# A softmax over 16 tiles: whole-tile passes, long multiplies, a later alignment, two stores from another issuer

## Chip, cores, metric

One core of one Trainium2 chip. The metric is the device time in microseconds (us) of one execution; medians over several executions are quoted.

Engine names as in the profile: DVE is VectorE, ACT is ScalarE, POOL is GpSimd, SP is SyncE; a q behind a name (SPq) is that engine's sequencer.

## The reference

```python
x = randn(32, 512, 1024) as float32        # 64 MiB in, 64 MiB out
scaled = x / 0.5
shifted = scaled - max(scaled, axis=-1)
out = exp(shifted) / sum(exp(shifted), axis=-1)
```

## The kernel before

The 16384 rows are 16 tiles of 128 partitions x 8 rows x 1024 elements, 4 MiB each, computed in place in six buffers. SP issues the loads, ACT the stores. Each tile is worked in two groups of four rows.

```python
TILES = [[8]] * 16
BUFS = 6
GROUP = 4
# ... cut: building the list of groups, the DRAM views
def load():                                # SP; waits until the buffer's old store has landed
    xt = data.tile([P, sum(TILES[i]), d], f32, name="xt")
    nc.sync.dma_start(out=xt, in_=dram(xf, i))
def maximum(g):                            # DVE
    nc.vector.tensor_reduce(out=top, in_=tiles[i][:, a : a + k, :], axis=X, op=extreme)
    nc.vector.tensor_scalar_mul(bias, in0=top, scalar1=-scale)
def exponential(g):                        # ACT, row by row, with the sum
    nc.scalar.activation(row, row, Exp, bias=bias[:, b : b + 1], scale=scale,
                         accum_out=sums[:, b : b + 1])
def divide(g):                             # DVE, row by row
    nc.vector.reciprocal(recip, sums)
    for b in range(k):
        nc.vector.tensor_scalar_mul(row, in0=row, scalar1=recip[:, b : b + 1])
def store(g):                              # ACT issues, once a tile
    nc.scalar.dma_start(out=dram(of, i)[:, a : a + k, :], in_=tiles[i][:, a : a + k, :])
    load()                                 # the load of tile i + 6

nc.vector.addr_align(128, offset=0, max_nops=0)
nc.scalar.addr_align(128, offset=0, max_nops=0)
for _ in range(BUFS):
    load()
for g in range(len(groups) + 1):           # one group ahead
    if g < len(groups):
        maximum(g); exponential(g)
    if g > 0:
        divide(g - 1); store(g - 1)
```

Of the kernel before, what the change touches and what calls it, by code (L numbers as in the profile page):

```python
# [1 line left out]

# [4 lines left out]



TILES = [[8]] * 16  # L10
BUFS = 6

GROUP = 4


@with_exitstack
def kernel(
    ctx: ExitStack,
    tc: tile.TileContext,
    x: bass.AP,  # L20
    temperature: bass.AP,
    out: bass.AP,
):
    nc = tc.nc
    f32 = mybir.dt.float32
    scale = 1.0 / float(temperature)
    extreme = mybir.AluOpType.max if scale > 0 else mybir.AluOpType.min

    P = 128
    xf = x.flatten_outer_dims()  # L30
    of = out.flatten_outer_dims()
    n, d = xf.shape
    assert sum(sum(ks) for ks in TILES) * P == n

    data = ctx.enter_context(tc.tile_pool(name="data", bufs=BUFS))
    stats = ctx.enter_context(tc.tile_pool(name="stats", bufs=4))


    groups, first, r = [], [], 0
    for i, ks in enumerate(TILES):  # L40
        first.append(r)
        r += sum(ks)
        a = 0
        for k in ks:
            for b in range(0, k, GROUP):
                m = min(GROUP, k - b)
                groups.append((i, a + b, m, (a, k) if b + m == k else None))
            a += k

    def dram(t, i):  # L50
        k = sum(TILES[i])
        block = t[P * first[i] : P * (first[i] + k), :]
        return block.rearrange("(p k) d -> p k d", p=P, k=k)

    tiles, small = [], []

    def load():
        i = len(tiles)
        if i < len(TILES):
            xt = data.tile([P, sum(TILES[i]), d], f32, name="xt")  # L60
            nc.sync.dma_start(out=xt, in_=dram(xf, i))
            tiles.append(xt)

    def maximum(g):
        i, a, k, _ = groups[g]
        top, bias, sums, recip = (
            stats.tile([P, k], f32, name=name) for name in ("top", "bias", "sums", "recip")
        )
        small.append((bias, sums, recip))
        nc.vector.tensor_reduce(  # L70
            out=top, in_=tiles[i][:, a : a + k, :], axis=mybir.AxisListType.X, op=extreme
        )
        nc.vector.tensor_scalar_mul(bias, in0=top, scalar1=-scale)  # L73

    def exponential(g):
        i, a, k, _ = groups[g]
        bias, sums, _ = small[g]
        for b in range(k):
            nc.scalar.activation(  # L79
                tiles[i][:, a + b, :],  # L80
                tiles[i][:, a + b, :],
                mybir.ActivationFunctionType.Exp,
                bias=bias[:, b : b + 1],
                scale=scale,
                accum_out=sums[:, b : b + 1],
            )

    def divide(g):
        i, a, k, _ = groups[g]
        _, sums, recip = small[g]  # L90
        nc.vector.reciprocal(recip, sums)  # L91
        for b in range(k):
            nc.vector.tensor_scalar_mul(  # L93
                tiles[i][:, a + b, :], in0=tiles[i][:, a + b, :], scalar1=recip[:, b : b + 1]
            )

    def store(g):
        i, _, _, part = groups[g]
        if part:
            a, k = part  # L100
            nc.scalar.dma_start(out=dram(of, i)[:, a : a + k, :], in_=tiles[i][:, a : a + k, :])
            if a + k == sum(TILES[i]):
                load()



    with tc.manual_schedule():

        nc.vector.addr_align(128, offset=0, max_nops=0)
        nc.scalar.addr_align(128, offset=0, max_nops=0)  # L110
        for _ in range(BUFS):
            load()
        for g in range(len(groups) + 1):
            if g < len(groups):
                maximum(g)
                exponential(g)
            if g > 0:
                divide(g - 1)
                store(g - 1)


# [1 line left out]
_INS = ['x', 'temperature']  # L123
_OUTS = [((32, 512, 1024), 'float32')]

_NUMBERS = {'temperature': 0.5}


# [26 lines left out]
```

## Time and profile before

| | before |
|---|---|
| median time | 317.70 us (317.50 to 317.98, 6 runs) |
| span of the profiled run | 315.6 us |
| DVE, ACT busy | 235.5 us, 149.6 us |
| DMA | 134.26 MB, 425 GB/s over the span |
| tile 15 lands, last store issued, last store landed | 282.23, 302.01, 314.82 us |

Read it from the DMA row down: the 16 DMA engines are at 9 tenths in 38 of the 40 slices, and DVE and ACT at 75% and 47% of the span.

### The profile page before, as it was taken

What the parts mean: (1) busy time and instruction counts of PE and PEld (TensorE: products, weight loads), DVE (VectorE), ACT (ScalarE), POOL (GpSimd) and SP (SyncE); (2) the same over time, 40 slices, a digit from 0 to 9 for tenths busy, and PEclk for the clock granted to TensorE, in tenths of its full rate; (3) what the DMA queues carried; (4) which work ended last, traced back from release to release, by engine and by line L of the source; (5) the groups of instructions that cost most, each with busy time, mean ns of one, the idle gap of its engine ahead of it and who ended that gap; (6) DMA issues with size and microseconds to landing.
All of it is one profiled execution on the core that took longest, in us unless ns stands there. A gap on an engine that the chain in (4) does not pass through costs nothing.

```text
span 315.6 us, 622 instructions
## 1 busy us (share of the span) xinstructions
DVE 235.5 (75%) x224; ACT 149.6 (47%) x257; POOL 0.2 (0%) x4
## 2 busy tenths in 40 slices
DVE  0299999999789494994939949498594976949720
ACT  0176666666626255361553615546065560645500
POOL 0000000000000000000000000000000000000000
DMA  8999999999999999999999999999999999999996
GB/s 330 415 448 415 386 457 407 461 411 453 424 440 432 432 432 429 444 424 453 415 454 407 457 407 457 403 461 403 461 403 461 403 462 403 461 419 444 428 436 278
DMA packets 4613, 134.26 MB, mean 425 GB/s; under 512 B 512, under 2 KB 512, under 8 KB 512
## 3 DMA queue, kind: packets, MB, share of 16 engines
q1 hardware_dynamic: 2304, 67.11, 49.7%
q10 hardware_dynamic: 2304, 67.11, 49.2%
q14 instruction: 5, 0.04, 0.0%
HBM read 67.11 MB, written 67.11 MB: 425 GB/s over the span
## 4 chain that ended last, share of the span: by engine, by line
DVE 72%; another core or an unknown queue 15%; DMA 4%; ACT 3%; issue 1%; DVEq 0%
DVE top L70 43%; DVE xt L93 27%; DMA xt<-in_x_dram 4%; ACT xt L79 3%; DVE recip L91 1%; DVE bias L73 1%; DVEq L150 0%
## 5 line engine op out<-in xcount | busy, mean ns | idle before, releaser
L79 ACT ACTIVATE xt<-xt,bias 128x1024 f32<-128x1024 f32 x128 | 145.4, 1137 | 136.0 <-DVE recip L91 118.6
L70 DVE TENSOR_REDUCE top<-xt 128x4 f32<-128x4096 f32 x32 | 141.3, 4416 | 62.2 <-DMA xt<-in_x_dram 62.2
L93 DVE TENSOR_SCALAR xt<-xt,recip 128x1024 f32<-128x1024 f32 x128 | 87.7, 749 | 1.1
L79 ACT ACTIVATION_READ_ACCUMULATOR xt<-xt,bias 128x1 f32 x128 | 23.8, 186 | 0.0
L79 ACT ACT_TABLE_LOAD x1 | 1.3, 1283 | 13.5 <-DMA xt<-in_x_dram 13.5
L91 DVE RECIPROCAL recip<-sums 128x4 f32<-128x4 f32 x32 | 5.5, 171 | 2.1 <-ACT xt L79 2.1
L73 DVE TENSOR_SCALAR bias<-top 128x4 f32<-128x4 f32 x32 | 5.5, 170 | 1.1
L136 POOL MEMSET const-bfloat16-1.0<- 128x1 bf16 x1 | 0.1, 102 | 0.0
L136 POOL MEMSET const-uint8-127<- 128x1 uint8 x1 | 0.1, 102 | 0.0
L136 POOL MEMSET const-float32-0.0<- 128x1 f32 x1 | 0.1, 99 | 0.2 <-issue 0.2
L136 POOL MEMSET const-float32-1.0<- 128x1 f32 x1 | 0.1, 99 | 0.0
## 6 DMA issues: line engine op xcount, KB each, us to landing
xt<-in_x_dram SPq DMA_DIRECT2D x16, 4096.0 KB, 50.2
out_dram<-xt ACTq DMA_DIRECT2D x16, 4096.0 KB, 38.4
```

The costliest lines, as they stand in the source:

```text
L70: nc.vector.tensor_reduce(out=top, in_=tiles[i][:, a : a + k, :], axis=mybir.AxisListType.X, op=extreme)
L73: nc.vector.tensor_scalar_mul(bias, in0=top, scalar1=-scale)
L79: nc.scalar.activation(tiles[i][:, a + b, :], tiles[i][:, a + b, :], mybir.ActivationFunctionType.Exp, bias=bias[:, b : b + 1], scale=scal ...
L91: nc.vector.reciprocal(recip, sums)
L93: nc.vector.tensor_scalar_mul(tiles[i][:, a + b, :], in0=tiles[i][:, a + b, :], scalar1=recip[:, b : b + 1])
L136: nc = _bacc.Bacc("TRN2", target_bir_lowering=False, num_devices=1)
```

## The change

The intent: fewer DVE instructions and waits (maximum over a whole tile in tiles 2 to 13; in six of these one long multiply by a broadcast operand in place of eight short ones), the two alignment instructions behind the fourth pass in place of the front, and the last two stores issued by SP, whose last load goes out at 231.9 us in the old trace.

```diff
-TILES = [[8]] * 16
-GROUP = 4
+PASSES = [[4, 4]] * 2 + [[8]] * 12 + [[4, 4]] * 2
+WHOLE = (3, 5, 7, 9, 11, 13)
+ALIGNED = 3
+BY_SP = 2
 ... (cut: the list of groups follows PASSES)
     def divide(g):
         nc.vector.reciprocal(recip, sums)
+        if i in WHOLE:
+            xt = tiles[i][:, a : a + k, :]
+            nc.vector.tensor_mul(xt, xt, recip.unsqueeze(2).to_broadcast([P, k, d]))
+            return
         for b in range(k):
             nc.vector.tensor_scalar_mul(...)
     def store(g):
-            nc.scalar.dma_start(...)
+        if a + k == ROWS:
+            queue = nc.scalar if i < len(PASSES) - BY_SP else nc.sync
+            queue.dma_start(out=dram(of, i), in_=tiles[i])
+            load()
     with tc.manual_schedule():
-        nc.vector.addr_align(128, offset=0, max_nops=0)
-        nc.scalar.addr_align(128, offset=0, max_nops=0)
         ...
                 store(g - 1)
+            if g == ALIGNED:
+                nc.vector.addr_align(128, offset=0, max_nops=0)
+                nc.scalar.addr_align(128, offset=0, max_nops=0)
```

More of the change, by code (lines that the diff above doesn't have):

```diff
@@ L6 @@
 from concourse._compat import with_exitstack
-TILES = [[8]] * 16
+ROWS = 8
 BUFS = 6
-GROUP = 4
+PASSES = [[4, 4]] * 2 + [[8]] * 12 + [[4, 4]] * 2
+WHOLE = (3, 5, 7, 9, 11, 13)
+ALIGNED = 3
+BY_SP = 2
 @with_exitstack
@@ L32 @@
     n, d = xf.shape
-    assert sum(sum(ks) for ks in TILES) * P == n
+    assert len(PASSES) * ROWS * P == n
     data = ctx.enter_context(tc.tile_pool(name="data", bufs=BUFS))
     stats = ctx.enter_context(tc.tile_pool(name="stats", bufs=4))
-    groups, first, r = [], [], 0
-    for i, ks in enumerate(TILES):
-        first.append(r)
-        r += sum(ks)
-        a = 0
-        for k in ks:
-            for b in range(0, k, GROUP):
-                m = min(GROUP, k - b)
-                groups.append((i, a + b, m, (a, k) if b + m == k else None))
-            a += k
+    groups = []
+    for i, ks in enumerate(PASSES):
+        assert sum(ks) == ROWS
+        for j, k in enumerate(ks):
+            groups.append((i, sum(ks[:j]), k))
     def dram(t, i):
-        k = sum(TILES[i])
-        block = t[P * first[i] : P * (first[i] + k), :]
-        return block.rearrange("(p k) d -> p k d", p=P, k=k)
+        block = t[P * ROWS * i : P * ROWS * (i + 1), :]
+        return block.rearrange("(p k) d -> p k d", p=P, k=ROWS)
     tiles, small = [], []
@@ L58, in load @@
         i = len(tiles)
-        if i < len(TILES):
-            xt = data.tile([P, sum(TILES[i]), d], f32, name="xt")
+        if i < len(PASSES):
+            xt = data.tile([P, ROWS, d], f32, name="xt")
             nc.sync.dma_start(out=xt, in_=dram(xf, i))
@@ L64, in maximum @@
     def maximum(g):
-        i, a, k, _ = groups[g]
+        i, a, k = groups[g]
         top, bias, sums, recip = (
@@ L75, in exponential @@
     def exponential(g):
-        i, a, k, _ = groups[g]
+        i, a, k = groups[g]
         bias, sums, _ = small[g]
@@ L88, in divide @@
     def divide(g):
-        i, a, k, _ = groups[g]
+        i, a, k = groups[g]
         _, sums, recip = small[g]
         nc.vector.reciprocal(recip, sums)
+        if i in WHOLE:
+            xt = tiles[i][:, a : a + k, :]
+            nc.vector.tensor_mul(xt, xt, recip.unsqueeze(2).to_broadcast([P, k, d]))
+            return
         for b in range(k):
@@ L97, in store @@
     def store(g):
-        i, _, _, part = groups[g]
-        if part:
-            a, k = part
-            nc.scalar.dma_start(out=dram(of, i)[:, a : a + k, :], in_=tiles[i][:, a : a + k, :])
-            if a + k == sum(TILES[i]):
-                load()
+        i, a, k = groups[g]
+        if a + k == ROWS:
+            queue = nc.scalar if i < len(PASSES) - BY_SP else nc.sync
+            queue.dma_start(out=dram(of, i), in_=tiles[i])
+            load()
     with tc.manual_schedule():
-        nc.vector.addr_align(128, offset=0, max_nops=0)
-        nc.scalar.addr_align(128, offset=0, max_nops=0)
         for _ in range(BUFS):
```

## The prediction

> **What bounds the kernel now.** I read the page's slices and DMA queues first, then the windows by stage, then the chain of waits, then the groups.
>
> From the page:
>
> ```profile
> span 315.6 us, 622 instructions
> DVE 235.5 (75%) x224; ACT 149.6 (47%) x257; POOL 0.2 (0%) x4
> ...
> DMA  8999999999999999999999999999999999999996
> ...
> DMA packets 4613, 134.26 MB, mean 425 GB/s; under 512 B 512, under 2 KB 512, under 8 KB 512
> q1 hardware_dynamic: 2304, 67.11, 49.7%
> q10 hardware_dynamic: 2304, 67.11, 49.2%
> q14 instruction: 5, 0.04, 0.0%
> ```
>
> No compute engine is full (DVE, VectorE, is busy 75% of the span), but the 16 DMA engines are at 9 tenths in every slice except the first and the last, and the loads (q1) and the stores (q10) together take 49.7 + 49.2 = 98.9% of them. That names the bound: bytes. Nothing in the program can remove bytes, since 67.11 MB must be read and 67.11 MB written.
>
> The windows by stage give the rate (columns: window, its length, busy time of DVE, ACT and POOL with their counts, clock, DMA share, GB/s):
>
> ```profile
> 14.00:32.00 18.00, 17.65 (x15) 11.65 (x20) 0.00 (x0) 1.00 1.01 437
> 32.00:40.00 8.00, 7.93 (x9) 5.25 (x11) 0.00 (x0) 1.00 1.00 389
> ...
> 88.00:282.00 194.00, 147.26 (x140) 92.74 (x160) 0.00 (x0) 1.00 1.01 434
> ```
>
> Loads alone run at 437 GB/s while DVE is busy 17.65 of 18 us, and loads mixed with stores run at 434. So the rate depends neither on the mix nor on what DVE does. Only the 8 us around the first store are slower, at 389: (434 - 389) / 434 of 8 us is 0.8 us lost.
>
> The chain of waits tells which engine waits in the steady part:
>
> ```profile
> 258.42 4.46 another core or an unknown queue
> ...
> 262.90 4.43 DVE top L70
> 267.35 0.17 DVE bias L73
> ...
> 282.25 4.43 DVE top L70
> ```
>
> DVE waits some 4.5 us for every tile, and tiles come 282.25 - 262.90 = 19.35 us apart. A tile is 4.194 MB in and 4.194 MB out; 8.389 MB in 19.35 us is 433.5 GB/s: the pace is the DMA's. The page's chain gives 72% to DVE, but that is only because it walks through an engine that itself waits for loads.
>
> The groups (count, then busy time and mean ns) give the durations that I use:
>
> ```profile
> L79 ACT ACTIVATE xt<-xt,bias 128x1024 f32<-128x1024 f32 x128 | 145.4, 1137 | 136.0 <-DVE recip L91 118.6
> L70 DVE TENSOR_REDUCE top<-xt 128x4 f32<-128x4096 f32 x32 | 141.3, 4416 | 62.2 <-DMA xt<-in_x_dram 62.2
> L93 DVE TENSOR_SCALAR xt<-xt,recip 128x1024 f32<-128x1024 f32 x128 | 87.7, 749 | 1.1
> ```
>
> [...] The trace shows that issue time as 0.34 us for a store. So moving two stores to SP (SyncE) is worth tenths at most. [...] four multiplies of 1024 elements take 2.74 us in the chain, 0.685 us each[...]. The new operation is in no trace yet[...]. [...] the store at 289.76 us was issued by ACT (ScalarE) before the last exponential of its group began (290.37).
>
> **The change part by part.**
> *Whole-tile passes (12 tiles).* A maximum over 8 rows replaces two over 4: 8192 elements in place of twice 4096. From the chain, 4.34 us for 4096, so about 8.6 to 8.75 for 8192; one bias and one reciprocal fewer a tile (0.17 + 0.09 us). DVE saves about 0.3 us a tile. But latency grows: the store of a tile now waits for the maximum of the whole next tile. Old: 4.43 + 0.17 + 0.09 + 2.74 = 7.4 us after the next tile's landing (7.5 in the trace, 282.25 to 289.76). New: 8.75 + 0.26 + 8 x 0.685 = 14.5 us[...].
> *Six tiles multiplied in one instruction.* 8.7 in place of 5.5 us: +3.2 us of DVE each, 19 us in all; the store of such a tile comes 8.75 + 0.26 + 8.7 = 17.7 us after the next landing.
> *Is DVE then the bound?* 14.5 us for plain tiles, 17.7 for the six, against tiles coming each 19.35 us: no. DVE's busy time becomes about 235.5 + 19 - 12 x 0.3 = 251 us.
> *Do buffers stall the loads?* A buffer's turn has 6 x 19.35 = 116 us. Held now: 19.35 (until the next landing) + 7.5 = 27 us; the rest, 89 us, is queueing in the two DMA queues (median 50.2 for a load, 38.4 for a store). New hold: 34 to 37 us, leaving 79 us or more, where a load and a store that share the engines need about 19.35 each. The queues get shorter but don't run dry.
> *Alignment and fewer instructions.* DVE runs 78 fewer: 12 x (1 reduction + 1 bias + 1 reciprocal) = 36, and 6 x 7 = 42 multiplies. The page has 5 instruction fetches of 8 KB (q14). Each takes one of the 16 engines for 8 KB at 434 / 16 GB/s = 0.3 us, and the slowest engine sets the end. One or two fewer: -0.3 to -0.6 us.
> *Last two stores by SP.* Same bytes, same engines: 0 to -0.3 us.
> *The first stores.* Old: store 0 issued at 33.1, store 1 at 47.9, and the load that waits for store 0 goes out at 57.3. So the store queue never ran dry. New: the first four passes are the old ones, then comes the maximum over 8 rows: 40.4 + 8.75 + 0.26 + 2.74 = 52.2 us[...]. That is just before store 0's end (57): most likely no gap; if there is one, the loads get the engines meanwhile, and only a second start of writing can cost its 0.8 us. I count a third of it, +0.2.
> *The tail.* If tile 15 still lands at 282.25: tile 14's four steps with tile 13's long multiply in between end at 262.90 + 4.43 + 0.26 + 8.7 + 4.34 + 0.26 + 2.74 = 283.6; then maximum, bias and reciprocal, multiply (7.34 us) to 291.0, maximum, bias, reciprocal and multiply again (7.34) to 298.3. The last exponentials end at about 300.2 and the last multiply, with its reciprocal, at about 303.1, where it was 302.0. Store 14 landed at 305.2 in the old trace, so the last store may be late by about a microsecond and still find the engines busy. And loads get ahead while early stores are later, so tile 15 should land up to 3 us sooner, which gives this back. Net 0.
> Sum: -0.45 - 0.1 + 0.2 + 0 = about -0.4 us: 317.7 - 0.4 = 317.3 us.
>
> **The rivals.**
> *DVE takes over.* For: +19 us of DVE work, and the catching-up between 13 and 85 us where DVE never waits. Against: 17.7 < 19.35. It would need a long multiply above 19.35 - 9.0 = 10.3 us[...]; at 13 us the six tiles would lose 6 x 2.7 = 16 us less the slack of the plain tiles (4.8 us each), so still only a few us: 319 to 322.
> *The tail opens.* The last store late by 2 to 3 us beyond what is queued: 319 to 320. For it: the shift of 1.1 us above. Against it: store 14's queue and the earlier loads.
> *A real gain.* The floor: 134.26 MB at 434 GB/s is 309.4 us; the first bytes come after some 1.5 us, and landing and closing take some 1.5 us: span 312.4, and 317.7 - 315.6 = 2.1 us lie outside the span: 314.5. That is 1.0% under now. A gain of over 2% (under 311.4) is not to be had without fewer bytes.
>
> **Range and chances.** 317.3 us; the sum's terms are each below a microsecond, the floor 314.5 closes it below, and the tail or the second start of writing can add 1 to 1.5: 316.0 to 318.8 for 8 in 10. Faster by over 2%: 0.01. Within 2%: 0.97. Slower by over 2% (above 324): 0.02[...].
>
> **What would show it.** Right: the DMA row stays at 9 throughout and the steady window at 434 GB/s; one group of six multiplies near 8.7 us; reductions of 128x8192 near 8.75; DVE near 251 us (80%) and still waiting for loads; stores issued 14 to 18 us after the next landing, landing sooner after issue than 38.4 us. Wrong: a slice at 8 or less in the DMA row between 40 and 300 us, SP waiting for stores with no load in flight, a gap between the landing of store 14 and the first bytes of store 15, or DVE without waits in the second half.

The sum: it came to -0.45 - 0.1 + 0.2 + 0 = -0.35, put as about -0.4 us, so 317.3 us. The 8.7 us for one long multiply, which is in the 17.7 us, in DVE's 251 us and in the tail, could not be had from the old trace (the changed kernel's shows 8692 ns). The -0.1 us for the last two stores is a guess beside the 0.34 us that issuing a store took in the trace. The floor holds for the measured 434 GB/s; that no more is to be had was not shown. Its two times of some 1.5 us are 1.74 us (the first data packet's start) and 1.1 us (315.6 - 314.47, from the last packet's end) in the old trace.

## More of the kernel before

All runs here were with a granted clock of 1.0.

"In the flow" means: while loads and stores keep all 16 DMA engines busy.

## The result, and the profile after

The changed kernel takes 318.23 us (317.78 to 318.49, 6 runs) where the old one takes 317.70. The ratio is 1.0014, 95% interval 1.0001 to 1.0027. Ratios here are the mean time of one kernel's fast runs over that of the other's in the same rounds, so not quite the ratio of the medians. It is the same within 2%, inside the predicted range, but on the other side: +0.5 us where -0.4 was predicted. The rest of this document is about that half microsecond; it is small, but most of it can be followed in the records.

The page of the changed kernel:

```profile
span 316.5 us, 534 instructions
DVE 250.8 (79%) x146; ACT 148.2 (47%) x257; POOL 0.2 (0%) x4
...
DMA  8999999999999999999999999999999999999996
...
q14 instruction: 5, 0.04, 0.0%
```

DVE has 15.3 us more work, and the DMA row is the same, digit for digit. There are 78 DVE instructions fewer, and still five instruction fetches.

Its windows by stage (window, length, busy time of DVE, ACT and POOL, clock, DMA share, GB/s):

```profile
32.00:40.00 8.00, 7.93 (x9) 5.25 (x11) 0.00 (x0) 1.00 1.00 385
...
88.00:282.00 194.00, 161.04 (x80) 87.89 (x153) 0.00 (x0) 1.00 1.01 434
```

The steady rate is 434 GB/s again. Nothing was gained or lost in those 194 us.

Its groups, shape by shape:

```profile
L70 DVE TENSOR_REDUCE top<-xt 128x8 f32<-128x8192 f32 x12 | 104.2, 8685 | 31.3 <-DMA xt<-in_x_dram 31.3
L94 DVE TENSOR_TENSOR xt<-xt,recip 128x8192 f32<-128x8192 f32 x6 | 52.1, 8692 | 0.2
```

Both durations are as forecast (8.6 to 8.75 us, from the old trace's 4.34 for half of it, and 8.7 us).

The end of its chain of waits (start, length, what):

```profile
258.24 4.92 another core or an unknown queue
...
263.19 4.43 DVE top L70
...
267.95 8.69 DVE xt L94
...
276.64 4.34 DVE top L70
...
284.03 4.34 DVE top L70
```

DVE waits for tile 14's landing (the 4.92 us), but not for tile 15's: that tile landed at 282.51, and its maximum starts at 284.03, because tile 13's 8.69 us stand in front. So the last store is issued at 303.63, where it was 302.01. The DMA engines notice. Microsecond by microsecond, before and then after:

```profile
303.00:304.00 1.00, 0.00 (x0) 0.00 (x0) 0.00 (x0) 1.00 1.22 524
304.00:305.00 1.00, 0.00 (x0) 0.00 (x0) 0.00 (x0) 1.00 1.14 492
```

```profile
303.00:304.00 1.00, 0.60 (x1) 0.00 (x0) 0.00 (x0) 1.00 0.31 131
304.00:305.00 1.00, 0.00 (x0) 0.00 (x0) 0.00 (x0) 1.00 1.22 524
```

A packet counts in the microsecond in which it starts, and takes 1.21 us; so shares go above 1, and a single thin microsecond can also be the space between two bunches of starts. The packet records settle it: from 302 to 309 us an engine idles 0.00 us on average before the change and 0.75 us after it, with only 3 of 16 engines active at the worst point. A gap near the very end, and 0.9 us more span: it looks like the whole explanation.

A second difference is quieter: where the instruction fetches (q14) fall. The queues in the first 10 us and from 10 to 313 us, before:

```profile
q1 hardware_dynamic: 110, 3.60, 89.9%
q14 instruction: 2, 0.02, 0.6%
...
q14 instruction: 3, 0.02, 0.0%
```

and after, for the same two stretches:

```profile
q1 hardware_dynamic: 108, 3.54, 88.7%
...
q14 instruction: 5, 0.04, 0.0%
```

Two of the five fetches have moved from the start into the flow, to 43.2 us. The trace shows the alignment as one branch instruction each on ACT and DVE: at 0.72 and 0.76 us before, at 37.42 and 37.50 after, some 6 us ahead of the two fetch packets.

### The profile page after: what moved, and what is told of

Read it like the earlier page. It is cut to its first block, busy times and chain, and to the rows that moved or that the text cites. A ratio compares the mean times of both kernels' runs of the same rounds, so it can differ in the third digit from the quotient of the medians.

```text
span 316.5 us, 534 instructions
## 1 busy us (share of the span) xinstructions
DVE 250.8 (79%) x146; ACT 148.2 (47%) x257; POOL 0.2 (0%) x4
## 4 chain that ended last, share of the span: by engine, by line
DVE 77%; another core or an unknown queue 11%; DMA 4%; ACT 3%; issue 1%; DVEq 0%; ACTq 0%
DVE top L70 43%; DVE xt L94 16%; DVE xt L97 16%; DMA xt<-in_x_dram 4%; ACT xt L79 3%; DVE recip L91 1%; DVE bias L73 1%; DVEq L154 0%; ACTq L154 0%
## 5 line engine op out<-in xcount | busy, mean ns | idle before, releaser
L70 DVE TENSOR_REDUCE top<-xt 128x8 f32<-128x8192 f32 (+1 forms) x20 | 139.5, 6976 | 49.4 <-DMA xt<-in_x_dram 49.4
L97 DVE TENSOR_SCALAR xt<-xt,recip 128x1024 f32<-128x1024 f32 x80 | 54.3, 748 | 0.5
L94 DVE TENSOR_TENSOR xt<-xt,recip 128x8192 f32<-128x8192 f32 x6 | 52.1, 8692 | 0.2
L91 DVE RECIPROCAL recip<-sums 128x8 f32<-128x8 f32 (+1 forms) x20 | 3.7, 185 | 2.0 <-ACT xt L79 2.0
L73 DVE TENSOR_SCALAR bias<-top 128x8 f32<-128x8 f32 (+1 forms) x20 | 3.4, 170 | 0.7
## 6 DMA issues: line engine op xcount, KB each, us to landing
out_dram<-xt ACTq DMA_DIRECT2D x14, 4096.0 KB, 28.8
```

What stands on the lines that cost most here:

```text
L94: nc.vector.tensor_mul(xt, xt, recip.unsqueeze(2).to_broadcast([P, k, d]))
L97: nc.vector.tensor_scalar_mul(tiles[i][:, a + b, :], in0=tiles[i][:, a + b, :], scalar1=recip[:, b : b + 1])
```

## The experiments

All runs gave correct results. They ran in three groups, in the order below (the first four, the next four, the last three), each with the old kernel beside it: its medians were 317.69, 317.72 and 317.81 us, so times from different groups compare to about 0.1 us.

**Theory T**: the gap in the tail. **Rival A**: the new issuer of the last stores. **Rival B**, later sharpened to **theory F**: the instruction fetches, which each set back one DMA engine, while the engine furthest back sets the end.

### Tile 13 short again (closes the gap)

```diff
-WHOLE = (3, 5, 7, 9, 11, 13)
+WHOLE = (3, 5, 7, 9, 11)
```

> The changed kernel with tile 13 multiplied by eight short instructions again (the other five long ones, SP's two stores and the moved alignment stay). Theory T (the tail: tile 13's long multiply, 8.69 us in place of 5.39, makes VectorE reach tile 15 at 284.0 us, 1.5 us after its landing at 282.5; so the last store is issued at 303.6 and the DMA engines idle about 1 us between stores 14 and 15): VectorE waits for tile 15 again, the last store goes out at 302.0 to 302.4, the window 303 to 304 us is full (over 400 GB/s, it was 131), and the time falls to 317.5 to 317.8, a ratio to before of 0.999 to 1.001. Rivals A (stores by SP) and B (alignment and instruction fetches): it stays at 318.2, ratio 1.0014.

Measured: 318.07 us, ratio to before 1.0011 (0.9999 to 1.0024). T misses. DVE waits for tile 15 again, and the microsecond from 303 is full:

```profile
303.00:304.00 1.00, 0.00 (x0) 0.00 (x0) 0.00 (x0) 1.00 1.15 492
304.00:305.00 1.00, 0.00 (x0) 0.00 (x0) 0.00 (x0) 1.00 0.15 66
```

The second line is mostly the space between two bunches: the packet records leave 0.25 us of idleness per engine, a third of the changed kernel's 0.75. It is not quite zero, as in this run tile 15 itself landed late, at 283.17, and the last store went out at 302.96. Taking away most of the gap gave 0.2 us at most, within the noise.

### The last two stores by ACT

```diff
-BY_SP = 2
+BY_SP = 0
```

> The changed kernel with the last two stores issued by ACT, as before. Theory T: the last store waits for VectorE's last multiply, whoever issues it, so it goes out at 303.6 plus or minus 0.2 us, the gap of about 1 us stays, and the time stays at 318.0 to 318.4. Rival A (a change of issuer[...] costs time): it falls to 317.7.

Measured: 318.30 us, ratio 1.0014 (1.0000 to 1.0027); the last store at 303.48. Rival A is out: the issuer is worth nothing that can be seen.

### Alignment at the front

```diff
     with tc.manual_schedule():
+        nc.vector.addr_align(128, offset=0, max_nops=0)
+        nc.scalar.addr_align(128, offset=0, max_nops=0)
 ...
-            if g == ALIGNED:
-                (both alignments)
```

> The changed kernel with the two alignment instructions at the front, as before. Theory T: the gap in the tail stays, time 318.0 to 318.4; the two instruction fetches seen at about 43 us move to the first 4 us. Rival B (placing of the fetches costs the time): it falls to 317.7 or moves by more than 0.4 us.

Measured: 317.74 us, ratio 0.9996 (0.9984 to 1.0009): the whole loss is gone. And the gap is still there, with the last store at 303.38:

```profile
303.00:304.00 1.00, 0.36 (x1) 0.00 (x0) 0.00 (x0) 1.00 0.16 66
```

The packet records have 0.64 us of idleness per engine, nearly the changed kernel's 0.75, and it costs nothing. T falls as the explanation of this half microsecond.

### Tile 14 long as well (a dose for the tail)

```diff
-WHOLE = (3, 5, 7, 9, 11, 13)
+WHOLE = (3, 5, 7, 9, 11, 13, 14)
```

> The changed kernel with tile 14 long as well (two instructions of 4 x 1024 elements, about 4.4 us each in place of 2.74). A dose: theory T says that each microsecond by which VectorE's last multiply is late beyond the edge is one microsecond of time. Both long multiplies stand before tile 15's last steps, +3.3 to +3.4 us: last store at about 307.0, DMA idle about 4.3 us, time 321.3 to 321.8. If the end were bound by bytes alone, or the gap in the trace were an accident of it: 318.2.

Measured: 321.29 us, ratio 1.0113; last store at 306.38, 2.75 us later than in the changed kernel, span 319.2, 2.7 us longer. So a late last store does cost, but only from some point on. The idleness is 2.32 us per engine here. The first part of a microsecond is free, as the run before showed. Something else was still busy then. That the 2.7 us match the 2.75 is partly chance: 15 engines end at 316.96 to 317.13 us and one at 317.93, and that one had a fetch at 308.80, in the middle of store 15.

### What was still busy: the slowest DMA engine

Each of the 16 engines (told apart by the chains described further down) moves eight 32 KB packets of every tile and then one packet of 4 bytes: the records before have 2048 + 2048 packets of 32 KB and 256 + 256 of 4 bytes for 16 loads and 16 stores. The spread of the 16 small packets of a transfer tells how far the last engine is behind the first. This table is worked out from the packet records of the traces, one profiled run each; the times are medians of unprofiled runs:

```
kernel                    fetches before    last engine behind     idle per engine,   time
                          10 us / later     the first when         302 to 309 us,     us
                                            store 14 ends, us      us
before                    2 / 3             1.42                   0.00               317.70
after                     0 / 5             2.17                   0.75               318.23
tile 13 short             0 / 5             2.09                   0.25               318.07
stores by ACT             0 / 5             2.34                   0.68               318.30
alignment at the front    2 / 3             1.45                   0.64               317.74
```

Now the gap is understood. In the changed kernel the first engine is done with store 14 at 303.4 us, the last one 2.17 us later, at 305.57. That one then needs 8 x 1.213 = 9.7 us for its share of store 15: 315.27, and its last packet ends at 315.26 in the trace. Most engines idle for a while, but the one that sets the end does not. In the kernel before, the same sum gives 303.4 + 1.42 + 9.7 = 314.5, and the trace has 314.47. The difference of 0.75 us is the loss in these two profiled runs, whose spans differ by 0.84 us; the medians differ by 0.53. Tile 14 long made the gap wider than that lag (2.32 us of idleness per engine), and only then did it cost.

The next runs test whether the fetches make the lag.

### A dose of fetches

The kernel with the alignment at the front, and on SP behind each of the last ten load issues 96 increments of a semaphore that nobody reads:

```diff
             tiles.append(xt)
+            if i >= BUFS:
+                for _ in range(96):
+                    nc.sync.sem_inc(filler)
```

> The changed kernel with the alignment at the front (as in the run e3_align_front, 317.74 us), and 96 semaphore increments that do nothing[...], on SP behind each of the last ten load issues: 960 instructions, so 7 or 8 more instruction fetches of 8 KB while loads and stores are in full flow. Theory F (each fetch puts one of the 16 DMA engines back by some 0.4 to 0.7 us, and the engine that is furthest back sets the end): if SP's fetches go to one engine, that one falls back by 3 us or more and the time is 319.5 to 322; if they are spread over the engines, 317.8 to 318.5. The share of the instruction queue grows from 5 to 12 or 13 packets, and the last slices get thinner. Rival T (only VectorE's last multiply and the gap before the last store count): 317.7, unchanged.

Measured: 323.62 us, ratio 1.0184 (1.0170 to 1.0198): the direction of F, and more than it expected. The run shows eight more for the 960 increments. From the page:

```profile
q14 instruction: 13, 0.11, 0.1%
```

Eight fetches more, 64 KB beside 134 MB, cost 323.62 - 317.74 = 5.9 us, 0.74 us each when all eight fall on one engine. The packet records show one engine falling back: 2.9 us behind the first at 124 us, 5.6 at 202, 7.4 at 284, while the second slowest stays at 1.9 to 2.3. SP's own time is not the cause: each load still goes out within 0.2 us of the landing of the store it waits for. A fetch packet takes 0.31 us, and the data packet next to it is often stretched from 1.21 to between 1.3 and 1.75 us; together (the fetch and the excess over 1.21) these are 0.4 to 0.85 us. A load's landing waits for that engine too: tile 15 landed at 287.04, and its store went out at 308.11, so part of the 5.9 us comes by way of a late last store.

### One part alone: the old kernel with the alignment moved

```diff
-        (both alignments at the front)
 ...
                 store(g - 1)
+            if g == 3:
+                nc.vector.addr_align(128, offset=0, max_nops=0)
+                nc.scalar.addr_align(128, offset=0, max_nops=0)
```

> The kernel before with nothing changed but the alignment, which moves behind the fourth pass. Theory F: the two fetches at 1.8 and 3.7 us[...] move to about 43 us, into the full flow; one or two engines fall behind by about half a microsecond more; time 318.0 to 318.3, although the last store is still issued at 302.0 and no gap opens. Rival T: 317.7, unchanged.

Measured: 318.27 us, ratio 1.0018 (1.0004 to 1.0032), as F expected. Its first 10 us hold no 8 KB fetch, and from 10 to 313 us there are five:

```profile
q14 instruction: 5, 0.04, 0.0%
```

Two of them fall at 43 us, and the last engine is 2.41 us behind at the end of store 14. One part of the expectation missed: tile 15 landed late, at 283.11, the last store went out at 302.90 and not at 302.0, and a gap of 0.34 us per engine opened. The moved alignment alone makes the whole loss, without whole-tile passes, long multiplies or SP's stores. Why the two fetches cost less in the first 4 us than at 43 us was not shown (the old trace has its first data packet at 1.74 us and the fetches at 1.76 and 3.60); that they do, this pair of kernels shows (317.72 and 318.27 us).

### The changed kernel without alignment

```diff
-            if g == ALIGNED:
-                nc.vector.addr_align(128, offset=0, max_nops=0)
-                nc.scalar.addr_align(128, offset=0, max_nops=0)
```

> The changed kernel without any alignment. Theory F: [...]3 to 5 instruction packets after 1 us; time 317.6 to 318.1, the lower the fewer of them fall after 10 us. Theory T: 318.2, as the gap in the tail stays.

Measured: 317.17 us, ratio 0.9981 (0.9969 to 0.9994): better than both kernels, and better than F's own range. How the alignment brings fetches about was not shown. Its instruction queue and the microsecond from 303:

```profile
q14 instruction: 3, 0.02, 0.0%
```

```profile
303.00:304.00 1.00, 0.16 (x1) 0.00 (x0) 0.00 (x0) 1.00 0.08 33
```

Three fetches in all, so the two alignments had brought two with them here (in the old kernel, below, it was one). The gap is still there (0.46 us per engine), and this is the lowest median, though the last two runs below are within its noise.

### Front alignment, fewest DVE instructions, no gap

```diff
-WHOLE = (3, 5, 7, 9, 11, 13)
+WHOLE = (2, 3, 4, 5, 6, 7, 8, 9, 10, 11, 12)
 (and the alignment at the front)
```

> Meant to beat both: alignment at the front, one long multiply for each of tiles 2 to 12 (fewest VectorE instructions, perhaps one fetch fewer), tile 13 short again so that the last store goes out at 302.0 to 302.4 without a gap. Theory F: the end is set by the DMA engine that lost most to fetches; as in before and in e3_align_front, 317.4 to 317.8, no gain from closing the gap alone. Theory T: closing the gap of 1 us gives 316.7 to 317.0.

Measured: 317.81 us, ratio 1.0001 (0.9988 to 1.0014); last store at 302.29, no gap. That is the edge of F's range, and far from T's. It was meant to win and does not: four fetches in place of five, and the last engine is still 1.47 us behind. The count alone doesn't decide.

### The old kernel without alignment

```diff
-        nc.vector.addr_align(128, offset=0, max_nops=0)
-        nc.scalar.addr_align(128, offset=0, max_nops=0)
```

> The kernel before without its two alignment instructions, nothing else. Theory F (fetches during the flow put single DMA engines back, 0.74 us each by the dose run, and the engine furthest back sets the end): the two alignments force two fetches, which go; 3 packets or so are left in the flow, as before (3 in the flow and 2 hidden at the front), so the time depends on which engines these fall on: 317.0 to 317.8. If the whole gain of the run without alignment came from the missing alignment: 317.1 to 317.4.

Measured: 318.11 us, ratio 1.0012 (0.9999 to 1.0024), a miss: slower than either range. It has four fetches, all in the flow (65.0, 65.4, 181.7 and 240.5 us), and a lag of 2.17 us. So leaving out the alignment is no gain in itself. In the old kernel it may have had one use: with it, two of five fetches fell into the first 4 us, and three came in the flow in place of four.

### Fewest fetches, no gap

```diff
-WHOLE = (3, 5, 7, 9, 11, 13)
+WHOLE = (2, 3, 4, 5, 6, 7, 8, 9, 10, 11, 12)
 (and no alignment)
```

> Meant to beat both: no alignment, long multiplies for tiles 2 to 12 (fewest VectorE instructions), tile 13 short (no gap in the tail). Theory F: 2 or 3 instruction packets in the flow; time 316.5 to 317.3. If the long multiplies themselves cost time, over 317.7.

Measured: 317.38 us, ratio 0.9989 (0.9976 to 1.0001), just above the range: three fetches, lag 1.13 us. Eleven long multiplies in place of six cost nothing that can be seen.

### No alignment, no gap

```diff
-WHOLE = (3, 5, 7, 9, 11, 13)
+WHOLE = (3, 5, 7, 9, 11)
 (and no alignment)
```

> The changed kernel without alignment (317.17 us in the run e7_no_align) and with tile 13 short, so that the last store goes out at about 302.2 and the gap of about 1 us in the tail closes. Theory F: the slowest DMA engine was 1.3 us behind the first one when store 15 began in e7_no_align, so the gap lay in the shadow of that engine; closing it gives nothing: 317.0 to 317.3. Theory T: 316.2 to 316.6.

Measured: 317.29 us, ratio 0.9986 (0.9972 to 1.0000). The last store goes out at 301.84 instead of 303.19, and the idleness falls from 0.46 to 0.00 us per engine:

```profile
303.00:304.00 1.00, 0.00 (x0) 0.00 (x0) 0.00 (x0) 1.00 1.14 492
```

Nothing is won: the last packet ends at 314.30 us here and at 314.31 in the changed kernel without alignment. That is F's range, and T is out a second time.

The rest of the table:

```
kernel                      fetches before 10 us / later   lag, us   idle, us   time, us
more fetches                2 / 11                         4.39      2.26       323.62
old kernel, alignment late  0 / 5                          2.41      0.34       318.27
no alignment                0 / 3                          1.34      0.46       317.17
front alignment, no gap     2 / 2                          1.47      0.00       317.81
old kernel, no alignment    0 / 4                          2.17      0.15       318.11
fewest fetches, no gap      0 / 3                          1.13      0.01       317.38
no alignment, no gap        0 / 3                          1.13      0.00       317.29
```

The idleness does not sort the times; the lag nearly does: 1.1 to 1.3 us for 317.2 to 317.4, 1.4 to 1.5 for 317.7 to 317.8, 2.1 to 2.4 for 318.1 to 318.3. (Two are left out of this: tile 14 long, where the gap decides, and the dose, where the laggard also made tile 15 and so the last store late.)

**Which engine carried a fetch.** The records do not name the DMA engine of a packet, but their times give it away: in the flow a packet starts 3 to 4 ns before the one ahead of it on its engine ends. So the packets can be strung into 16 chains, one for each engine. The check: 12 of the 13 runs give 256 data packets in every chain, as 16 loads and 16 stores of eight packets must (the run with tile 13 short has one pair of chains mixed up). This is what the chains show (the last packet's end in us):

```
kernel                    engine with fetches at               ends at            engines without a fetch
before                    3.60, 162.34                         314.47             313.05 to 313.54,
                          1.76, 124.63, 253.33                 314.40             and one 314.34
changed                   43.22, 152.04, 286.93                315.26             314.21 to 314.38
                          43.27, 299.98                        315.16
old, alignment late       43.23, 201.94                        315.34             313.49 to 313.71
                          43.15, 160.23, 281.80                315.00
more fetches              SP's eight, 66.40 to 247.17          320.57             318.70 to 318.85
```

In all 13 runs the engine that ends last is one that carried fetches. That is theory F seen directly. The added fetches of SP all went to one engine; the others went to two more.

**What stays open.** The number of fetches does not give the lag: two in the flow on the last engine came with 1.13 us (no alignment, no gap), 1.34 (no alignment), 2.17 (old kernel, no alignment) and 2.41 (alignment late). Nor is every lag a fetch's: one engine of the old kernel ended 1.3 us late without any, and in the changed kernel the spread of 2.13 us at the end of store 0 was that of an engine without a fetch (the two with one stood at 0.90 and 0.70), whose load packets were stretched when writing started at 33 to 38 us (from 32 to 40 us single load packets took 1.3 to 2.0 us, one 2.8, in place of 1.21, and the DMA moved 385 GB/s, 389 before the change). That early lag was gone by the end of store 12. What makes such lags go, and why a data packet behind a fetch is stretched by 0.1 us or by 0.5, no run here shows.

## Why the prediction was right and wrong

- *The bound* was right: 434 GB/s in the steady part in both kernels, the same DMA row, and 15.3 us more DVE work with 0.5 us more time.
- *The parts on DVE* were right: 8692 ns, 8685 ns, 250.8 us in all. Stores go out 14.5 us after the next landing for a plain tile (88.55 to 103.03) and 17.8 for a long one (107.90 to 125.73); their landing takes a median of 28.8 us in place of 38.4.
- *The first stores* were right: store 1 at 51.91 us, before store 0 landed (57.79). No second start of writing.
- *The tail* was right in its sum and wrong in its reason. The last store was put at 303.1 and came at 303.6. "Tile 15 should land up to 3 us sooner" failed: it landed at 282.51, where it was 282.23. Loads kept their half of the engines and did not get ahead: in the chains, from 60 to 275 us the next packet is of the other queue in 98.7% of cases before the change and 99.6% after it. A gap opened, and it cost nothing for a reason that the prediction did not have: it lay behind the slowest engine. Closing it moved the time by -0.2 us in one pair (318.23 to 318.07) and +0.1 in the other (317.17 to 317.29).
- *Alignment and fewer instructions* is the step that failed. It said one or two fetches fewer, -0.3 to -0.6 us. There were five before and after, and two of them moved from the start into the flow: +0.5 us, which the old kernel with nothing but the moved alignment shows by itself (318.27 us). The prediction's notion that a fetch delays one engine and the slowest sets the end was right, but it priced a fetch at its own 0.3 us, where the dose gave 0.74, and it did not price the diff's moved lines at all. Without alignment, where the fetches differ in number, the times do too: the old kernel has four fetches and the changed one three (318.11 and 317.17 us, each against before in its own rounds: 1.0012 and 0.9981).
- *The number* lay in the range although its sign was wrong, and that is no credit to the sum: the range was 2.8 us wide, and the whole change moved the time by 0.5. In the floor, 2.1 us outside the span should have been 1.8, as the profiled run took 317.42 us for its 315.6; so 314.2 in place of 314.5, and nothing hangs on it.

## What to carry to other kernels

In a kernel whose DMA engines are full from end to end, as here (9 tenths in 38 of 40 slices), look for the engine that ends last, not for the average: in the changed kernel it ended at 315.26 us, and 14 of the 16 by 314.38; in the dose, 8 KB of instructions, added to an engine that thereby became the last, cost 0.74 us, the time of 20 KB of data at that engine's share of 434 / 16 = 27 GB/s. A visible gap at the end of a trace need not be a cost: 0.64 us of idleness per engine came with 317.74 us here, no gap with 317.70, and 2.32 us with 321.29; close it in an experiment before believing in it. The alignment instructions, one branch each on ACT and DVE in the trace, moved two instruction fetches to 43 us here and, in the changed kernel, came with five in place of three, so a list of instructions that got shorter should be tried without them.
